# The modulation's sums: one operation of 1024 columns each, and 26 instead of 16 of them in the first feed-forward

## The chip, the cores and the metric

One core of one Trainium2 chip. The metric is the device time of one execution in microseconds, the median of several runs.

## What is computed

Two blocks of a model run one after the other on 256 tokens of width 1024, all in float32. The first block has two layers (pooling and attention, then a gated recurrence), each followed by a feed-forward with a short convolution. The second block has four mixers side by side and a feed-forward, and its two normalised inputs and its two outputs are scaled and shifted by six vectors of width 1024, the modulation, which depend on one row `c` alone:

```python
c_act = jax.nn.silu(c.astype(jnp.float32))
...
mod = (c_act @ ada_w[l] + ada_b[l])[:, None, :]
sh1, sc1, gt1, sh2, sc2, gt2 = jnp.split(mod, 6, axis=-1)
h = rms_norm_2(x, norm_mix_g[l]) * (1.0 + sc1) + sh1
...
x = x + gt1 * (merged @ w_o[l])
h = rms_norm_2(x, norm_ffn_g[l]) * (1.0 + sc2) + sh2
x = x + gt2 * (jnp.square(jax.nn.relu(h @ ffn_w1[l])) @ ffn_w2[l])
```

The product `c_act @ ada_w` has 6144 results of 1024 terms each. It is not made on TensorE: with 128 results on the partitions, 48 columns of sums are made on VectorE (DVE), each the sum of a weight row times `c_act`.

## The kernel before

**Weights.** All weights of the matrix products come in one stream of chunks of 16 tiles of 128 x 128 (1 MB each), loaded by SyncE's queue (`w_dma`, L212) into three buffers. Every product is made in three matmuls of halves of the precision (`mm3`, L276 to L282): high weight by high input, high by low, low by high. The halves of the weights are made on the way (`w_split`, L226): for each 8 tiles ScalarE (ACT) copies the raw weights rounded into `hi` (L246) and DVE subtracts that from the raw ones into `lo` (L247, by the helper L322). There are five pairs of `hi` and `lo` buffers, and the splits run four packages of 8 tiles ahead of their use, `W` (L257) asking for them.

**Order.** The program is one list of work; each engine runs its own part in order. The order among DVE's operations is partly pinned (`behind`, L289): what `step` and `ada_step` issue stays behind what DVE was given before. The stages are mixer 0 (to about 100 us), the first feed-forward (about 100 to 300 us), mixer 1, the second feed-forward (about 390 to 580 us), the four mixers, the last feed-forward. `ffn` (L871) makes 22 groups of 16 tiles; after each, `evac` (L876) applies the convolution, the gelu and the split on ACT and DVE. From the eighth group on, 8 tiles of the output product follow each group, for the group seven before.

**The sums.** `ada_load` (L443) loads 1 MB of modulation weights, two columns of sums, into one of three large buffers, on SyncE's queue, pinned behind what stands there. `ada_step` (L453) makes one column: two scalar_tensor_tensor operations of 512 columns, each with its sum into `macc` (L461). After every second step the next load is issued, but not after steps 28, 30, 32 and 40. `W` calls a step once for every 16 tiles while fewer than `ada_to` steps are done: from the fifth group of the first feed-forward to 16 steps (`ADA_B`, L904), from the fifth group of the second to 32, in the mixers to 38 and 40, in the last feed-forward to 48. `ada_finish` (L468) adds the two halves and the bias for what is used next.

**The set-up of the S5 mixer** (`s5_setup`, L1085) runs in small parts, one for each group of the second feed-forward, called by `step`: small operations on DVE, a Sin on ACT (L1121), six operations of 256 columns on DVE (L1148 to L1150), and once 32 steps of the sums are done, the tables of cosines and sines on GpSimd (POOL, L1170 to L1184), with eight doublings of their length, from 8 to 1024 columns an operation. The tables lie in the three large buffers of the sums' weights. They are read much later, in the mixers.

**Arena.** `al` and `fr` (L162, L179) hand out 46 slots of 512 columns in turn. `start_small` (L512) puts the row `c_act` (doubled) into two of them, which it keeps until the last feed-forward.

Of the kernel before, what the change touches and what calls it, by code (L numbers as in the profile page):

```python
# [12 lines left out]
OP = mybir.AluOpType  # L13
# [11 lines left out]
N_TILES = (128 + 4 + 64 + 2 * (352 + 176) + 160 + 80 + 408 + 3 * 16 + 32 + 64 + 256 + 256)  # L25
TPC = 16
N_CHUNK = -(-N_TILES // TPC)
N_SLOT = 46
MAGIC = 12582912.0
SUM_AT, SPREAD_AT = 6, 2  # L30
SB = 3
# [1 line left out]
STEPS0 = (3, 7)  # L33
ADA_P = 4
SIDE = 4
ADA_B = 16
ADA_M = 38
AHEAD = ((4, 1), (8, 8), (4, 1), (4, 1), (4, 1), (4, 1))
S5_C = 2
# [97 lines left out]
class Prog:  # L137
    def __init__(self, ctx, tc, args):
# [14 lines left out]
        self.uid = self.nsp = 0  # L153
        self.slots = deque(range(N_SLOT))
        self.held = {}
# [120 lines left out]
    def mm3(self, out, key, x, start, stop):  # L276

        wh, wl = self.W(key)
        mm = self.nc.tensor.matmul
        mm(out, wh, x[0], start=start, stop=False, skip_group_check=True)  # L280
        mm(out, wh, x[1], start=False, stop=False, skip_group_check=True)  # L281
        mm(out, wl, x[0], start=False, stop=stop, skip_group_check=True)  # L282

    def mm(self, out, l, r, start=True, stop=True):
        self.nc.tensor.matmul(out, l, r, start=start, stop=stop, skip_group_check=True)  # L285
# [167 lines left out]
    def ada_step(self):  # L453

        i = self.ada_done
        self.ada_done += 1
        raw = self.ada_raw[i // 2]
        with self.behind(*PINNED):
            for h in range(2):
                x = raw[:, (i % 2) * 1024 + h * 512:(i % 2) * 1024 + h * 512 + 512]  # L460
                self.nc.vector.scalar_tensor_tensor(x, x, 0.5, self.cs[h], op0=OP.mult, op1=OP.mult,  # L461
                                                    accum_out=self.macc[:, h, i:i + 1])
        if i % 2 == 1:
            del self.ada_raw[i // 2]
            if self.ada_done not in (28, 30, 32, 40):
                self.ada_load()

    def ada_finish(self, e):  # L468

        while self.ada_done < e:  # L470
            self.ada_step()
        b = self.ada_end
        self.ada_end = e
        c = self.mod[:, b:e]
        self.tt(c, self.macc[:, 0, b:e], self.macc[:, 1, b:e], OP.add)
        self.tt(c, c, self.pvs("adab")[:, b:e], OP.add)


    def start(self):
        nc, a = self.nc, self.a  # L480
        eps, one = self.cst([128, 1], "eps"), self.cst([128, 1], "one")
        nc.vector.memset(eps, EPS)
        nc.scalar.activation(one, eps, AF.Tanh)
        self.eps = eps
        warm = self.al()
        nc.vector.memset(warm[:, :T], 0.0)
        wb = self.bk()
        for _ in range(NWARM):
            self.mm(wb[:, :T], warm[:, :128], warm[:, :T])
        self.bf(wb)  # L490
        self.fr(warm)
        self.pvt = self.cst([128, NPV - PV0], "pvt")
        self.xp = self.cst([128, PV0 + KD * T], "xp")
        self.X = self.xp[:, PV0:].rearrange("p (k t) -> p k t", k=KD)
        p = 0
        for e in (1, 2, 4, 6, 8):
            q = PV0 + e * T
            nc.scalar.dma_start(out=self.xp[:, p:q], in_=a["xt"][:, p:q])
            p = q
        for c in range(self.NRAW):  # L500
            self.w_dma(c)
        cb = self.cst([128, 512], "cb")
        nc.sync.dma_start(out=cb, in_=a["cb"])
        nc.sync.dma_start(out=self.pvt, in_=a["pv"])
        self.ident, self.ones = cb[:, 0:128], cb[:, 128:256]
        self.bd, self.bdm = cb[:, 256:384], cb[:, 384:512]
        self.eps64 = self.cst([128, 1], "eps64")
        nc.vector.memset(self.eps64, 64e-5)
        self.xgh = self.cst([128, KD, T + 4], "xgh", F32R)
        self.macc, self.mod = self.cst([128, 2, 48], "macc"), self.cst([128, 48], "mod")  # L510

    def start_small(self):  # L512

        self.cs = []
        th = self.al()
        for h in range(2):
            c = self.al()
            self.nc.sync.dma_start(out=c, in_=self.a["crow"][:, h * 512:h * 512 + 512].to_broadcast([128, 512]))
            self.nc.scalar.activation(th, c, AF.Tanh, scale=0.5)
            self.stt(c, th, 1.0, c, OP.add, OP.mult)  # L520
            self.cs.append(c)
        self.fr(th)


# [346 lines left out]
    def ffn(self, l):  # L871
# [29 lines left out]
        for p, b in self.in_gen(specs, hs):  # L901
            evac(p, b)
            if p == ADA_P:
                self.ada_to = (ADA_B, 32)[l]  # L904
            if p == SIDE:
# [872 lines left out]
    def ffn2(self):  # L1778
        nc = self.nc
        hs = []  # L1780
        b3 = (128, 2, T)
        ys = {}
        specs = [[("ffn1", 2 * q), ("ffn1", 2 * q + 1)] for q in range(16)]

        def evac(q, b):
            r = self.al()
            nc.scalar.activation(r, b, AF.Relu)
            self.rel(b)
            h, l = self.al(F32R), self.al(F32R)
            nc.scalar.activation(h, r, AF.Square)  # L1790
            self.tt(r, r, r, OP.mult)
            self.tt(l, r, h.bitcast(F32), OP.subtract)
            self.fr(r)
            ys[q] = (h, l)

        def xk(q, i):
            return tuple(t[:, i * T:i * T + T] for t in ys[q])
        gate = lambda m: self.mod[:, 40 + m:41 + m]

        def out(q):  # L1800
            if q == 0:
                self.acc_begin()
            for i in range(2):
                self.out_k("ffn2", 2 * q + i, xk(q, i), q == 0 and i == 0)
            self.fr(*ys.pop(q))
        for q, b in self.in_gen(specs, hs):
            evac(q, b)
            if q == 4:
                self.ada_load(3)
                self.ada_to = 48  # L1810
            if LAG2 <= q and q - LAG2 < 16 - LAST2:
                out(q - LAG2)
        self.fr(*hs)
        for q in range(16 - LAG2, 16 - LAST2):
            out(q)
        self.ada_finish(48)
        self.fr(*self.cs)

        self.tb = [[self.bk() for _ in range(2)] for _ in range(2)]

        def turn(m):
            x = self.al()
            nc.scalar.activation(x[:, :T], self.X[:, m, :], AF.Copy, scale=self.pv("gfin", m))
            for h in range(2):
                nc.tensor.transpose(self.tb[h][m // 4][:, (m % 4) * 128:(m % 4) * 128 + 128],  # L1825
                                    x[:, h * 128:h * 128 + 128], self.ident)
            self.fr(x)
        with self.behind(ENG.Activation):
            self.nc.scalar.activation(self.cst([128, 1], "sqrt"), self.eps, AF.Sqrt)
        last = range(16 - LAST2, 16)  # L1830
        self.out_last("ffn2", range(32 - 2 * LAST2, 32), [xk(q, i) for q in last for i in range(2)], gate=gate,
                      after=turn)
        for q in last:
            self.fr(*ys.pop(q))
# [149 lines left out]
```

## Time and profile before

| | us |
|---|---|
| median of three runs | 1043.2 |
| lowest and highest | 1041.69 and 1044.56 |
| the profiled execution | 1046.05 |
| its span, first to last instruction | 1044.3 |
| TensorE (PE) busy | 1015.2 |
| DVE busy | 865.7 |
| ACT busy | 605.3 |
| POOL busy | 96.8 |

The granted clock of TensorE is 0.995 of full speed over the span, the 2.4 GHz level. A busy time counts an engine's instructions from start to end; consecutive ones can overlap a little. A wait in the profile is idle time of an engine just before an instruction, put down to what released it. Lines such as L322 and L331 are helpers that many places call, so tiles tell more: `lo<-raw,hi` is a split, `ada<-ada,s` a sum, `tab` a table, `s` an arena slot, `b` a PSUM bank.

### The profile page before, as it was taken

What the parts mean: (1) busy time and instruction counts of PE and PEld (TensorE: products, weight loads), DVE (VectorE), ACT (ScalarE), POOL (GpSimd) and SP (SyncE); (2) the same over time, 40 slices, a digit from 0 to 9 for tenths busy, and PEclk for the clock granted to TensorE, in tenths of its full rate; (3) what the DMA queues carried; (4) which work ended last, traced back from release to release, by engine and by line L of the source; (5) the groups of instructions that cost most, each with busy time, mean ns of one, the idle gap of its engine ahead of it and who ended that gap; (6) DMA issues with size and microseconds to landing.
All of it is one profiled execution on the core that took longest, in us unless ns stands there. A gap on an engine that the chain in (4) does not pass through costs nothing. (4 is left out here: it accounts for less than half of the span.)

```text
span 1044.3 us, 21508 instructions
## 1 busy us (share of the span) xinstructions
PE 1015.2 (97%) x8834; PEld 980.9 (94%) x8834; DVE 865.7 (83%) x1662; ACT 605.3 (58%) x953; POOL 96.8 (9%) x86
## 2 busy tenths in 40 slices
PE   9999999999999999999999999889999999999996
PEld 8879999999999999999999998778999999999996
DVE  6887999997799998999999978997667979775554
ACT  6566665565669975665654687233345457444444
POOL 0000000000000000000295000334200200000000
PEclk9999999999999999999999999999999999999999
DMA  8953367886682263777654644234454464955531
GB/s 310 353 186 119 125 207 272 305 314 223 211 281 95 71 235 120 241 255 269 225 202 153 241 149 149 72 116 146 145 198 162 154 206 142 386 172 192 191 133 41
DMA packets 32499, 202.75 MB, mean 194 GB/s; under 512 B 3601, under 2 KB 5137, under 8 KB 9233
## 3 DMA queue, kind: packets, MB, share of 16 engines
q1 hardware_dynamic: 31392, 199.80, 54.2%
q10 hardware_dynamic: 1008, 1.58, 0.4%
q8 instruction: 69, 1.13, 0.4%
q14 instruction: 30, 0.24, 0.1%
HBM read 200.32 MB, written 1.05 MB: 193 GB/s over the span
## 5 line engine op out<-in xcount | busy, mean ns | idle before, releaser
L281 PE MATMUL b<-s,hi 128*128 128x256 f32 x2192 | 616.9, 282 | 1.8 <-DVE s L331 0.9
L280 PE MATMUL b<-s,hi 128*128 128x256 f32 x2128 | 600.6, 283 | 4.8 <-ACT s L342 3.0
L282 PE MATMUL b<-s,lo 128*128 128x256 f32 x2128 | 598.2, 282 | 4.1 <-DVE lo L322 4.0
L322 DVE TENSOR_TENSOR lo<-raw,hi 128x1024 fp32r<-128x1024 f32 (+1 forms) x309 | 389.8, 1266 | 112.1 <-ACT hi L246 111.2
L246 ACT CAST hi<-raw 128x1024 fp32r<-128x1024 f32 (+1 forms) x309 | 319.8, 1041 | 261.4 <-PE b L281 185.4
L281 PEld LDWEIGHTS b<-s,hi 128*128 128x128 f32 x2192 | 413.4, 189 | 6.0 <-issue 3.0
L280 PEld LDWEIGHTS b<-s,hi 128*128 128x128 f32 x2128 | 400.6, 189 | 12.2 <-issue 4.0
L282 PEld LDWEIGHTS b<-s,lo 128*128 128x128 f32 x2128 | 400.9, 189 | 6.8 <-DVE lo L322 5.8
L322 DVE TENSOR_TENSOR s<-s,s 128x256 f32<-128x256 f32 (+3 forms) x173 | 89.2, 524 | 8.0 <-ACT s L373 3.7
L331 DVE SCALAR_TENSOR_TENSOR s<-b,pvt,s 128x255 f32<-128x255 f32 (+1 forms) x153 | 72.6, 478 | 3.8 <-ACT s L880 2.8
L461 DVE SCALAR_TENSOR_TENSOR ada<-ada,s 128x512 f32<-128x512 f32 x96 | 63.9, 685 | 3.6 <-DMA ada<-in_ada_dram 3.6
L285 PE MATMUL b<-xgh,hi 128*128 128x256 f32 (+1 forms) x212 | 60.5, 285 | 0.0
L285 PE MATMUL b<-s,hi 128*128 128x256 f32 x212 | 59.6, 281 | 0.0
L285 PE MATMUL b<-xgh,lo 128*128 128x256 f32 (+1 forms) x212 | 59.6, 281 | 0.0
L342 ACT CAST s<-s 128x256 fp32r<-128x256 f32 (+1 forms) x77 | 33.0, 440 | 37.0 <-DVE s L322 26.6
L880 ACT ACTIVATE s<-b,pvt 128x256 f32<-128x256 f32 x76 | 42.0, 556 | 8.5 <-PE b L282 8.2
L285 PE MATMUL b<-s,s 128*128 128x256 f32 (+5 forms) x212 | 39.2, 380 | 7.9 <-DVE s L322 7.4
L1174 POOL MEMSET tab<- 128x8 f32 x1 | 0.1, 113 | 494.2 <-DVE ada L461 494.2
L285 PEld LDWEIGHTS b<-s,hi 128*128 128x128 f32 x212 | 40.1, 189 | 0.0
L285 PEld LDWEIGHTS b<-xgh,lo 128*128 128x128 f32 x212 | 40.0, 189 | 0.0
L285 PEld LDWEIGHTS b<-xgh,hi 128*128 128x128 f32 x212 | 39.9, 188 | 0.0
L322 DVE TENSOR_TENSOR s<-s 128x256 f32<-128x256 f32 (+3 forms) x70 | 35.4, 508 | 4.7 <-ACT s L1790 4.3
(367 smaller groups left out, 1042.3 us busy)
## 6 DMA issues: line engine op xcount, KB each, us to landing
raw<-in_wst_dram SPq DMA_DIRECT2D x157, 1024.0 KB, 5.0
ada<-in_ada_dram SPq DMA_DIRECT2D x24, 1024.0 KB, 7.4
raw<-in_wst_dram SPq DMA_DIRECT2D x4, 512.0 KB, 6.4
s<-in_catt_dram SPq DMA_DIRECT2D x8, 192.0 KB, 7.2
s<-in_rgw_dram SPq DMA_DIRECT2D x5, 256.0 KB, 3.7
raw<-in_wst_dram SPq DMA_DIRECT2D x4, 256.0 KB, 5.5
xp<-in_xt_dram ACTq DMA_DIRECT2D x3, 256.0 KB, 6.1
s<-in_cinv_dram SPq DMA_DIRECT2D x2, 256.0 KB, 5.5
```

Source lines behind the costliest of these rows:

```text
L246: self.nc.scalar.copy(h, s)
L280: mm(out, wh, x[0], start=start, stop=False, skip_group_check=True)
L281: mm(out, wh, x[1], start=False, stop=False, skip_group_check=True)
L282: mm(out, wl, x[0], start=False, stop=stop, skip_group_check=True)
L285: self.nc.tensor.matmul(out, l, r, start=start, stop=stop, skip_group_check=True)
L322: self.nc.vector.tensor_tensor(out, a, b, op=op)
L331: self.nc.vector.scalar_tensor_tensor(out, a, s, b, op0=op0, op1=op1)
L342: nc.scalar.copy(hi, src)
L461: self.nc.vector.scalar_tensor_tensor(x, x, 0.5, self.cs[h], op0=OP.mult, op1=OP.mult, accum_out=self.macc[:, h, i:i + 1])
L880: nc.scalar.activation(c[:, i, :], z, AF.Identity, scale=self.pv(f"fcw{l}2", m), bias=self.pv(f"fcb{l}", m))
L1174: g.memset(S[:, :, 0:1], 0.0)
```

## The change

Each step makes one operation of 1024 columns with one sum, instead of two of 512; `macc` has one column a step, and the addition of the halves goes. The row `c_act` lies in one buffer of 1024 columns outside the arena, which has 44 slots instead of 46. `ADA_B` is 26: the first feed-forward makes steps 0 to 25, and the second 26 to 31. All sixteen loads that were issued up to step 26 are so issued in the first feed-forward, and the second issues none.

```diff
-N_SLOT = 46
+N_SLOT = 44
...
-ADA_B = 16
+ADA_B = 26
...
         with self.behind(*PINNED):
-            for h in range(2):
-                x = raw[:, (i % 2) * 1024 + h * 512:(i % 2) * 1024 + h * 512 + 512]
-                self.nc.vector.scalar_tensor_tensor(x, x, 0.5, self.cs[h], op0=OP.mult, op1=OP.mult,
-                                                    accum_out=self.macc[:, h, i:i + 1])
+            x = raw[:, (i % 2) * 1024:(i % 2) * 1024 + 1024]
+            self.nc.vector.scalar_tensor_tensor(x, x, 0.5, self.cs, op0=OP.mult, op1=OP.mult,
+                                                accum_out=self.macc[:, i:i + 1])
...
-        self.tt(c, self.macc[:, 0, b:e], self.macc[:, 1, b:e], OP.add)
-        self.tt(c, c, self.pvs("adab")[:, b:e], OP.add)
+        self.tt(c, self.macc[:, b:e], self.pvs("adab")[:, b:e], OP.add)
...
-        self.macc, self.mod = self.cst([128, 2, 48], "macc"), self.cst([128, 48], "mod")
+        self.macc, self.mod = self.cst([128, 48], "macc"), self.cst([128, 48], "mod")
...
-        self.cs = []
+        self.cs = self.cst([128, 1024], "cs")
         th = self.al()
         for h in range(2):
-            c = self.al()
+            c = self.cs[:, h * 512:h * 512 + 512]
...
-            self.cs.append(c)
...
-        self.fr(*self.cs)
```

## Rows read from the trace of the kernel before

**Rows 1.** busy time of the engines over the whole span

```profile
PE 1015.2 (97%) x8834; PEld 980.9 (94%) x8834; DVE 865.7 (83%) x1662; ACT 605.3 (58%) x953; POOL 96.8 (9%) x86
```

**Rows 2.** by stretch, us: busy PE, PEld, DVE, ACT, POOL; clock, DMA share

```profile
160.00:226.00 66.00, 66.00 (x559) 66.00 (x560) 65.16 (x142) 37.86 (x57) 0.00 (x0) 1.00 0.83 294
...
226.00:280.00 54.00, 54.00 (x459) 54.00 (x459) 41.56 (x62) 31.34 (x46) 0.00 (x0) 1.00 0.68 234
...
458.00:494.00 36.00, 34.71 (x290) 34.10 (x289) 33.90 (x87) 22.50 (x33) 0.00 (x0) 1.00 0.79 274
...
537.00:565.00 28.00, 28.00 (x239) 28.00 (x239) 27.58 (x22) 12.03 (x17) 26.47 (x14) 1.00 0.45 155
```

**Rows 3.** what PE waited for, 120 to 300 us (total, times, longest)

```profile
PE b L282 <- DVE lo L322: 1.3, 1, 1.3
```

**Rows 4.** the same view, 400 to 580 us

```profile
PE b L282 <- DVE lo L322: 1.7, 3, 0.9
...
PE b L280 <- ACT s L342: 1.0, 1, 1.0
...
PE b L281 <- DVE s L322: 0.7, 1, 0.7
```

**Rows 5.** timeline of DVE, second feed-forward: start us, us, engine, line

```profile
461.84 1.22 DVE L322 TENSOR_TENSOR lo<-raw,hi 128x1024 fp32r<-128x1024 f32 x1
462.97 0.48 DVE L331 SCALAR_TENSOR_TENSOR s<-b,pvt,s 128x254 f32<-128x254 f32 x1
463.36 0.68 DVE L461 SCALAR_TENSOR_TENSOR ada<-ada,s 128x512 f32<-128x512 f32 x1
...
463.97 0.69 DVE L461 SCALAR_TENSOR_TENSOR ada<-ada,s 128x512 f32<-128x512 f32 x1
...
464.58 1.22 DVE L322 TENSOR_TENSOR lo<-raw,hi 128x1024 fp32r<-128x1024 f32 x1
```

**Rows 6.** timeline: two splits on DVE and the matmul that first uses each

```profile
459.07 1.22 DVE L322 TENSOR_TENSOR lo<-raw,hi 128x1024 fp32r<-128x1024 f32 x1
...
460.83 0.28 PE L282 MATMUL b<-s,lo 128*128 128x256 f32 x1
...
491.36 1.22 DVE L322 TENSOR_TENSOR lo<-raw,hi 128x1024 fp32r<-128x1024 f32 x1
...
494.49 0.28 PE L282 MATMUL b<-s,lo 128*128 128x256 f32 x1
```

**Rows 7.** timeline: last sum of the sixth step; the Sin that the tables read

```profile
458.18 0.69 DVE L461 SCALAR_TENSOR_TENSOR ada<-ada,s 128x512 f32<-128x512 f32 x1
...
462.75 0.33 ACT L1121 ACTIVATE s5sa<-s5sa 128x144 f32<-128x144 f32 x1
```

**Rows 8.** timeline of POOL: memset of the cosines, a middle and the last table operation

```profile
514.88 0.11 POOL L1173 MEMSET tab<- 128x8 f32 x1 [9.77 <-DVE ada L461]
...
545.95 2.88 POOL L1179 TENSOR_TENSOR tab<-tab,s5sa 128x1024 f32<-128x1024 f32 x1
...
561.41 2.45 POOL L1184 TENSOR_TENSOR tab<-tab,tab 128x1024 f32<-128x1024 f32 x1
```

**Rows 9.** timeline of DVE and PE beside the tables

```profile
540.83 1.82 DVE L322 TENSOR_TENSOR lo<-raw,hi 128x1024 fp32r<-128x1024 f32 x1
...
551.24 0.28 PE L282 MATMUL b<-s,lo 128*128 128x256 f32 x1
...
543.59 1.49 DVE L322 TENSOR_TENSOR s<-s 128x256 f32<-128x256 f32 x1
...
561.53 3.41 DVE L322 TENSOR_TENSOR lo<-raw,hi 128x1024 fp32r<-128x1024 f32 x1
...
565.44 0.28 PE L282 MATMUL b<-s,lo 128*128 128x256 f32 x1
```

**Rows 10.** timeline of DVE: first and last of six operations of the set-up

```profile
484.73 0.42 DVE L322 TENSOR_TENSOR s<-s,s5qr 128x256 f32<-128x256 f32 x1
...
487.88 0.42 DVE L322 TENSOR_TENSOR s<-s,s 128x256 f32<-128x256 f32 x1
```

## The prediction

> **What bounds the kernel now.** I read the busy line first. TensorE is busy for 1015.2 of the 1044.3 us of the profiled span [rows 1], so the whole stock of idle PE time is some 29 us, and an edit on another engine can only move what PE waits for. The waits of PE come next, in the two stretches where the sums of the modulation lie: 1.3 us in the first feed-forward [rows 3], and 1.7, 1.0 and 0.7 us around the second [rows 4]. Then the busy time by stretch: beside the sums DVE is busy for 65.16 of 66 us and PE still runs without a gap; after them, 226 to 280 us, DVE is busy for 41.56 of 54 [rows 2]. The last thing I read is how early DVE delivers. DVE makes the low half ("lo") of eight weight tiles at a time; PE uses such a package in 24 matmuls. 459 matmuls in 54 us are 118 ns each [rows 2], so a package lasts 2.83 us and a step of the sums (every 16 tiles) comes every 5.65 us. The **lead** is the time from the end of a lo to the first matmul that loads it; I found that matmul by counting every eighth lo matmul back or on from one that waited for its lo. When the lead is used up, PE stops, one for one.
>
> **The operation itself.** Two halves of 512 columns start 0.61 us apart, and 0.61 us after the second the next work starts [rows 5]: 1.22 us a step, the reading of the accumulator included. The nearest row to one operation of 1024 columns with two SBUF operands is the lo itself: 1.13 us from its start to that of the next [rows 5]. I add 0.01 for the accumulator and take 1.14, with 1.13 and 1.22 as ends. That saves 0.08 us in each of 48 steps, 3.8 us of DVE time, at most a few tenths on the path: PE waits for DVE near few of these steps. The Trainium skill speaks against this form: "Vector Engine (DVE) Microarchitecture Reference", section "Points that are easy to get wrong", says that a scalar_tensor_tensor with two SBUF sources that are not bf16 runs at half throughput. The trace disagrees: a half of 512 columns takes 0.61 us where 1024 columns of the lo take 1.13, the same rate. By the rule a step would be 2.3 us and ten more would overfill the first feed-forward; I give it 1 in 100.
>
> **First feed-forward.** It gets ten more steps, 10 x 1.14 = 11.4 us of DVE work over 56.5 us, in the stretch where DVE idled for 12.4 of 54 us [rows 2]. It becomes as full as 160 to 226 us was, where PE lost nothing [rows 2]. So I cost it at nothing; the cover is the 12.4 us of idle DVE time, and what is left over is 1.0 us. If it is too thin, the nearest price is the 1.3 us that PE lost where the sums met the small set-up of the next mixer [rows 3]. The steps bring five loads of 1 MB with them, which move here from the second feed-forward. Each waits on SP's queue for the second sum of its pair, with the weight loads queued behind it. That is the pattern of 160 to 226 us too, at a DMA share of 0.83 against 0.68 after it [rows 2], without a wait of PE: nothing. The 1.3 us in this part I leave standing.
>
> **Second feed-forward.** It keeps six steps of sixteen. Ten steps of 1.22 us leave DVE. What PE lost there falls into two parts: 0.9 us at 484 and 0.4 at 488 us, where the sums met the set-up of the S5 tables on DVE (two of the three waits that make the 1.7), and 1.0 + 0.7 us at its end, where DVE came late out of the building of the tables [rows 4]. The third, the other 0.4, lies before the first step and stays. So 3.0 us can be won.
>
> But the sums also hold back **POOL**. The sine and cosine tables are written into the very buffers that the sums read, and POOL's memset of the cosines, behind which all but three tiny table operations stand, waited for the last sum of the sixteenth step, until 514.88 us [rows 8]. With six steps that sum ends near 458.9 us, and the tables then wait only for the Sin that they read, which ends at 463.08 us [rows 7]. So the tables start some 51.8 us earlier, and run through 463 to 512 us where they ran from 515 to 564. That matters, because beside POOL's operations the operations of DVE that read two SBUF operands stretch: a lo took 1.82 and 3.41 us instead of 1.22, and one of 256 columns 1.49 instead of 0.42 [rows 9, 10]. The Trainium skill has this rule: "SBUF — State Buffer", section "Who interferes with whom", says that a DVE instruction with two SBUF inputs and a GpSimd instruction that reads SBUF contend, and that the second to issue blocks until the first ends. The trace agrees: a lo of 1.22 us took 3.41 while POOL's operations of 2.45 and more ran.
>
> The lead, step by step. (1) The lo that ends at 460.29 us is used at 460.83: 0.54 us. The lo that ends at 492.58 is used at 494.49: 1.91 us [rows 6]. Between them PE waited 1.3 us [rows 4], so DVE just kept pace (1.91 - 0.54 - 1.3 = 0.07) while it did five steps of 1.22 us, the sums of 463.4 to 489 us. Without these 6.1 us the lead at the same place is 0.54 + 0.07 + 6.1 = 6.7 us, had POOL been quiet. (2) POOL's operations of 256 and 512 columns now fall there (they ran in the 15 us up to 545.95). Ordinary DVE work paid some five times 0.6 us for them (the lo of 540.83 [rows 9]): 3.0. The set-up's six operations of 256 columns, at 484.7 to 488.3 us [rows 10], now stand beside them too. No row shows these two together; the ends are nothing (they slip ahead of the larger operations) and 6 x 1.07 = 6.4 us (each paying as the one at 543.59 [rows 9]). Three of the six lie, shifted, among the 512-column operations; at 0.6 to 1.07 us each I take 2.6. Lead before the largest operations: 6.7 - 3.0 - 2.6 = 1.1 us, with 3.7 and below zero as ends. (3) The operations of 1024 columns: before, the lo that ended at 542.65 was used at 551.24, a lead of 8.6; the one that ended at 564.94 was used at 565.44, a lead of 0.5 [rows 9]. They cost 8.1 us, and a full lead just carried it. With 1.1 us of lead, PE waits 7.0 us, some time in 495 to 520 us; the ends are 8.1 - 3.7 = 4.4 and 8.1 + 6.4 - 3.7 = 10.8.
>
> After that DVE has neither sums nor POOL beside it, catches up in the rest of this part, and the last 1.7 us of waiting go. What is late next is nothing new: the end of the second feed-forward runs as that of the first did, with no wait of PE [rows 3].
>
> **The rest.** The row of conditioning values moves from two arena slots to a buffer of its own while the arena loses two: 44 slots are free either way from there on. One addition of at most 32 columns goes from each of four finishes. In the mixer and the second half of the model the steps stay where they were, 0.08 us shorter. All nothing, with 0.3 us either way.
>
> **Sum.** Waits lost 3.0, waits gained 7.0: +4.0 us. The profiled execution took 1046.05 us, its span 1044.3; by its own time the changed kernel would take 1050.1. It lies 2.85 us above the median of the three timed runs, 1043.2, so on that scale I forecast **1047.2 us**, with 1044.6 to 1051.0 from the ends. A measurement of this kernel can tell about 0.3%, 3.1 us, from no change: the bounds are 1040.1 and 1046.3.
>
> **Rivals.** (a) *The lead is full before the tables get heavy.* If the relieved DVE climbs to some 8 us of lead by 494 us, as it had in 537 us, it pays the 8.1 us from that and PE waits for almost nothing: 1043.2 - 3.0 = 1040.2, and some tenths less with the shorter operations. For it: DVE loses 6.1 us of work there. Against it: six set-up operations and the smaller POOL operations eat 3 to 6 of that. It decides at a lead of 8 us. (b) *Half of it.* The set-up slips ahead of the larger operations and PE waits 3 to 4.4 us: 1043.2 to 1044.6. (c) *The tables don't start earlier*, because POOL waits for something that the sums hid. Then only the 1.3 us at 484 and 488 us go and the end stays as it is: 1041.9. The trace shows nothing for such a wait, nor can it. (d) *The first feed-forward overflows*: the leftover of 1.0 us of idle DVE time is too little, weights come late, and PE pays 1.3 us or more there, on top of the forecast: 1048.5.
>
> **How the numbers follow.** Forecast 0.48 (a quarter of it under 1046.3), (a) 0.14, (b) 0.17, (c) 0.11, (d) 0.09, the half-rate operation 0.01. Slower by over 0.3%: three quarters of 0.48, and (d) and the half rate, 0.46, and a little for what no row shows: 0.49. Faster by over 0.3%: most of (a), 0.10. Within: 0.41. The range leaves out the ends of (a) and of the forecast: 1040.6 to 1050.0.
>
> **What would show it.** Right: the table operations on POOL from about 463 us; lo operations of 2 to 3.4 us in 494 to 512; a wait of PE for lo of some 7 us in 485 to 520; none at 565 to 570; PE without a gap in 226 to 280 with DVE busy for about 53 of 54 us; one sum of about 1.2 us by its duration, 48 of them. Wrong: POOL starting after 500 us, or the large table operations met by a lead of 8 us, or a new wait of PE at the end of the first feed-forward.

## The result, and the profile after

The changed kernel takes 1050.81 us (median of 13 runs, 1047.39 to 1056.07); the kernel before, run beside it on the same chip, 1044.56 us (13 runs, 1041.58 to 1048.48). The ratio is 1.0063, with 1.0049 to 1.0077 as its 95% interval: slower by some 6.6 us. The forecast was slower by 4.0 us, 1047.2; the time lies above the upper end of the range, 1050.0. (By the ratio alone it would be 1043.2 x 1.0063 = 1049.8 on the scale of the forecast, at the very end of the range.) The profiled execution of the changed kernel took 1051.49 us, its span 1049.7, 5.4 more than before.

The first lines of the page, and its group of the sums:

```profile
span 1049.7 us, 21408 instructions
...
PE 1018.3 (97%) x8834; PEld 985.2 (94%) x8834; DVE 862.9 (82%) x1563; ACT 605.3 (58%) x953; POOL 93.2 (9%) x86
...
L460 DVE SCALAR_TENSOR_TENSOR ada<-ada,cs 128x1024 f32<-128x1024 f32 x48 | 58.4, 1216 | 3.8 <-DMA ada<-in_ada_dram 3.8
```

DVE has 99 instructions and 2.8 us less than in [rows 1], and there are 48 sums of 1.22 us, as the change says. PE has the same 8834 matmuls and is busy 3.1 us *longer*. That is the first sign of something that the waits of PE will not show. The waits of PE, in 120 to 300, 300 to 400 and 400 to 600 us (total, times, longest), answer [rows 3, 4]:

```profile
PE b L280 <- DVE xp L322: 1.0, 1, 1.0
...
PE b L285 <- DVE s L322: 0.7, 1, 0.7
...
PE b L282 <- DVE lo L322: 4.1, 3, 2.7
PE b L280 <- ACT hi L246: 1.0, 1, 1.0
```

The wait of 1.3 us at 158 us is gone; two new ones of 1.0 and 0.7 stand at 290 and 301 us, where the first feed-forward ends and mixer 1 begins. In the second feed-forward PE waits 5.1 us, where it waited 3.4 [rows 4]. The busy time by stretch, with the columns of [rows 2]:

```profile
160.00:226.00 66.00, 66.00 (x561) 66.00 (x560) 64.89 (x118) 38.19 (x57) 0.00 (x0) 1.00 0.84 303
226.00:280.00 54.00, 54.00 (x459) 54.00 (x458) 47.92 (x77) 29.13 (x44) 0.00 (x0) 1.00 0.84 301
280.00:302.00 22.00, 20.28 (x171) 19.89 (x169) 20.51 (x38) 18.45 (x35) 0.00 (x0) 1.00 0.77 281
460.00:496.00 36.00, 36.00 (x308) 36.00 (x307) 36.00 (x65) 20.27 (x30) 31.63 (x43) 1.00 0.60 209
494.00:503.00 9.00, 6.31 (x53) 6.10 (x53) 9.00 (x10) 2.70 (x5) 8.92 (x5) 1.00 0.21 77
503.00:506.42 3.42, 3.42 (x18) 3.42 (x17) 3.42 (x3) 0.00 (x0) 3.34 (x2) 0.50 0.83 287
506.42:513.25 6.83, 4.37 (x33) 3.75 (x32) 6.12 (x7) 2.75 (x4) 3.54 (x2) 1.00 0.02 10
513.25:516.66 3.41, 3.41 (x18) 3.41 (x18) 3.30 (x7) 2.06 (x4) 0.00 (x0) 0.50 0.81 257
516.66:530.00 13.34, 13.34 (x114) 13.34 (x114) 13.13 (x21) 10.25 (x16) 0.00 (x0) 1.00 0.74 252
```

Read the column of the clock, last but two: right behind each stretch in which PE stood still (6.31 of 9 us, then 4.37 of 6.83) the granted clock is 0.50, the 1.2 GHz level, for 3.41 us. PE counts as busy for all of it. The timeline of PE, two matmuls inside the first fall and two behind it, gives the price:

```profile
504.09 0.41 PE L281 MATMUL b<-s,hi 128*128 128x256 f32 x1
504.30 0.41 PE L282 MATMUL b<-s,lo 128*128 128x256 f32 x1
...
506.55 0.28 PE L281 MATMUL b<-s,hi 128*128 128x256 f32 x1
506.67 0.28 PE L282 MATMUL b<-s,lo 128*128 128x256 f32 x1
```

Inside the fall a matmul starts every 0.213 us, outside every 0.118 us. Sixteen start in a fall (the 18 of the view count those that reach in from its ends), so each fall costs some 1.5 us, and the two 3.0 us. The kernel before has no such fall between 120 and 600 us.

POOL, from its memset of the cosines on, answers [rows 8] (timeline: start us, us, engine, line):

```profile
459.73 0.11 POOL L1170 MEMSET tab<- 128x8 f32 x1 [23.29 <-DVE ada L460]
463.36 0.21 POOL L1176 TENSOR_TENSOR tab<-tab,s5sa 128x8 f32<-128x8 f32 x1 [3.52 <-DMA raw<-in_wst_dram]
...
499.35 2.08 POOL L1179 TENSOR_TENSOR tab<-tab,s5sa 128x1024 f32<-128x1024 f32 x1
501.38 3.35 POOL L1178 TENSOR_TENSOR tab<-tab,tab 128x1024 f32<-128x1024 f32 x1
504.81 1.90 POOL L1180 TENSOR_TENSOR tab<-tab,s5sa 128x1024 f32<-128x1024 f32 x1
506.79 3.25 POOL L1181 TENSOR_TENSOR tab<-tab,tab 128x1024 f32<-128x1024 f32 x1
```

and DVE beside it, which answers [rows 9, 10]:

```profile
483.19 2.02 DVE L322 TENSOR_TENSOR s<-s,s 128x256 fp32r<-128x256 f32 x2
...
491.17 0.89 DVE L322 TENSOR_TENSOR mod<-macc,pvt 128x32 f32<-128x32 f32 x1
...
499.59 2.91 DVE L322 TENSOR_TENSOR lo<-raw,hi 128x1024 fp32r<-128x1024 f32 x1
502.43 0.47 DVE L331 SCALAR_TENSOR_TENSOR s<-b,pvt,s 128x255 f32<-128x255 f32 x1
502.82 1.94 DVE L358 CAST xgh<-mod 128x8 fp32r<-128x8 f32 x1
504.67 0.47 DVE L331 SCALAR_TENSOR_TENSOR s<-b,pvt,s 128x254 f32<-128x254 f32 x1
505.07 2.72 DVE L322 TENSOR_TENSOR lo<-raw,hi 128x1024 fp32r<-128x1024 f32 x1
507.71 2.61 DVE L322 TENSOR_TENSOR s<-s 128x256 f32<-128x256 f32 x1
```

Lay the two over each other. The lo of 499.59 ends at 502.50, 1.07 us after the POOL operation that was running when it came (499.35 + 2.08 = 501.43). The lo of 505.07 ends at 507.79, 1.08 us after its POOL operation (506.71). The CAST of eight columns a partition ends at 504.76, 0.03 us after its own (504.73), and the operation of 507.71 ends 0.28 us after 510.04. So each of them waits for the whole rest of the POOL operation in front of it and then takes its ordinary time. In the operations of 254 and 255 columns, which read one operand from PSUM, nothing stretches: 0.47 us.

By matching the same matmul in both traces, the 5.4 us of span arise so. At the start of the second feed-forward the changed kernel is 1.84 us behind; at its end (613.85 us before, 620.59 after) 6.74; the rest gives 1.3 back. The second feed-forward thus costs 4.9: waits 5.1 instead of 3.4, so 1.7; two falls of the clock, 3.0; 0.2 that I can't assign. The 1.84 ahead of it are 1.0 + 0.7 of new waits, less the 1.3 at 158 us, and 1.5 of a fall of the clock at 62.7 us (together 1.9). That fall is not the change's: nothing is changed there, and it comes and goes among the traces of this study (7 of 13 have it, one of them of a kernel that runs as the kernel before up to 493 us).

### The profile page after: what moved, and what is told of

It reads as the page before. It is cut to its first block, busy times and chain, and to the rows that moved or that the text cites. A ratio compares the mean times of both kernels' runs of the same rounds, so it can differ in the third digit from the quotient of the medians.

```text
span 1049.7 us, 21408 instructions
## 1 busy us (share of the span) xinstructions
PE 1018.3 (97%) x8834; PEld 985.2 (94%) x8834; DVE 862.9 (82%) x1563; ACT 605.3 (58%) x953; POOL 93.2 (9%) x86
## 3 DMA queue, kind: packets, MB, share of 16 engines
q8 instruction: 69, 1.13, 0.4%
## 5 line engine op out<-in xcount | busy, mean ns | idle before, releaser
L322 DVE TENSOR_TENSOR s<-s,s 128x256 fp32r<-128x256 f32 (+3 forms) x173 | 87.6, 514 | 6.3 <-ACT s L373 3.7
L460 DVE SCALAR_TENSOR_TENSOR ada<-ada,cs 128x1024 f32<-128x1024 f32 x48 | 58.4, 1216 | 3.8 <-DMA ada<-in_ada_dram 3.8
L322 DVE TENSOR_TENSOR s<-s 128x256 f32<-128x256 f32 (+3 forms) x70 | 37.7, 541 | 4.5 <-ACT s L1787 4.2
```

The lines of the kernel that those rows point to most:

```text
L322: self.nc.vector.tensor_tensor(out, a, b, op=op)
L460: self.nc.vector.scalar_tensor_tensor(x, x, 0.5, self.cs, op0=OP.mult, op1=OP.mult, accum_out=self.macc[:, i:i + 1])
```

## The experiments

My theory: the relieved sums let POOL build the tables inside the busiest part of the second feed-forward, DVE is held up by each large POOL operation, and PE stops. Against it stood that the added steps in the first feed-forward, or the operation of 1024 columns, cost the time. Waits are those of PE in the profiled execution, us; falls those of the granted clock between 490 and 530 us.

| | us | ratio to before | 120–300 | 300–400 | 400–600 | falls |
|---|---|---|---|---|---|---|
| before | 1043.7 to 1044.6 | 1 | 1.3 | 0 | 3.4 | 0 |
| changed | 1050.81 | 1.0063 (1.0049–1.0077) | 1.0 | 0.7 | 5.1 | 2 |
| e1 one operation, 16 steps | 1042.95 | 0.9988 (0.9975–1.0000) | 0 | 0 | 1.4 | 0 |
| e2 two halves, 26 steps | 1052.04 | 1.0080 (1.0060–1.0101) | 2.3 | 0.7 | 6.0 | 2 |
| e4 no tables | 1042.69 | 0.9986 (0.9975–0.9997) | 1.2 | 0.7 | 0 | 0 |
| e3 tables late, failed | 1048.34 | 1.0046 (1.0029–1.0062) | 0.8 | 0.7 | 5.6 | 2 |
| e7 tables late | 1042.42 | 0.9986 (0.9977–0.9996) | 0.3 | 0.7 | 0 | 0 |
| e5 tables in pieces | 1042.46 | 0.9983 (0.9971–0.9994) | 0.3 | 0.7 | 0 | 0 |
| e8 pieces, 16 steps | 1040.64 | 0.9974 (0.9964–0.9985) | 0 | 0 | 0 | 0 |
| e6 before, with pieces | 1041.82 | 0.9979 (0.9968–0.9990) | 0 | 0 | 0.4 | 0 |
| e10 pieces, 22 steps | 1041.68 | 0.9980 (0.9970–0.9991) | 0 | 0 | 0 | 0 |
| e9 finish kept in place | 1049.35 | 1.0055 (1.0035–1.0075) | 0.3 | 0.7 | 3.5 | one, 6.8 us |
| e11 no set-up operations | 1044.96 | 1.0011 (1.0001–1.0022) | 0 | 1.1 | 2.4 | 0 |

The runs of e1 to e5 and e7 to e9 had a kernel before of 1043.7 us beside them, those of e6, e10 and e11 one of 1044.11; compare by the ratio.

**Which part of the change (e1, e2).** e1 is the changed kernel with 16 steps:

```diff
-ADA_B = 26
+ADA_B = 16
```

> The changed kernel with 16 steps in the first feed-forward again: the one operation of 1024 columns, the row outside the arena and 44 slots stay. Theory T (the loss comes from the S5 tables on POOL, which start 50 us earlier when only six steps are left in the second feed-forward): ratio to before 0.998 to 1.001, the tables start at about 515 us, PE waits near 484 and near 568 us as before. Rival R1 (the longer operation or the moved row delays DVE): ratio 1.004 to 1.008.

e2 is the kernel before with 26:

```diff
-ADA_B = 16
+ADA_B = 26
```

> The kernel before with 26 steps in the first feed-forward and the two halves kept. Theory T: ratio 1.004 to 1.008, the tables start near 463 us and PE waits 4 to 7 us between 490 and 515. Rival R1: ratio 0.998 to 1.002.

e1 takes 0.9988 of before, e2 1.0080. The whole loss is in the move of the ten steps; the operation of 1024 columns is at most a small gain, for its interval reaches 1.0000. e1's waits did not stay where I expected them: the 1.4 us lie at 450, 456 and 567 us, and none near 484.

**Are the tables the cost (e4)?** The changed kernel fills both tables with constants and leaves the doublings on POOL out (its scan is not the model's):

```diff
-        g.memset(C[:, :, 0:1], 1.0)
-        g.memset(S[:, :, 0:1], 0.0)
-        for n in range(8):
+        g.memset(C[:, :, :], 1.0)
+        g.memset(S[:, :, :], 0.0)
+        for n in range(0):
```

> The changed kernel with the tables set by two memsets of their whole length; the doublings on POOL are left out. Theory T: no wait of PE from 430 to 600 us, ratio 0.995 to 0.999, and no fall of the granted clock near 500 us. Rival R2: ratio 1.003 to 1.007.

0.9986, no wait of PE in the second feed-forward and no fall of the clock there. So the tables in their new place cost 1.0063 - 0.9986 = 0.0077, 8.0 us (give or take 1.9, by the two intervals), and all the rest of the change is worth 1.5 us.

**Is it where they run (e3, e7)?** e3 wanted to hold the tables back with a small POOL operation that reads a late result of the feed-forward:

```diff
+            self.last_x = x[:, 0, :8].bitcast(F32)
...
+        late = self.cst([128, 8], "late")
+        g.tensor_tensor(late, self.last_x, self.last_x, op=OP.mult)
...
         g.memset(C[:, :, 0:1], 1.0)
```

> The changed kernel, but POOL must read an input of the output product of the group just evacuated before it builds the tables, so that they start near 510 us again; the 26 steps stay in the first feed-forward. Theory T: the waits of PE at 495 to 515 us go, none or less than 2 us at the end of the second feed-forward, ratio 0.996 to 1.001. Rival R2 (the fuller first feed-forward, or the order of DVE's work, costs the time): ratio stays at 1.004 to 1.007.

It failed as an experiment: nothing tied the tables to that operation, the memsets and the doublings went ahead of it, and the tables started at 462.46 us, the operation only at 516.00. What it gives is the changed kernel a second time, 1.0046. e7 keeps the order on POOL:

```diff
+            self.last_x = x[:, 0, :8].bitcast(F32)
...
-        g.memset(C[:, :, 0:1], 1.0)
-        g.memset(S[:, :, 0:1], 0.0)
+        late = self.cst([128, 8], "late")
+        g.tensor_tensor(late, self.last_x, self.last_x, op=OP.mult)
+        with self.behind(ENG.Pool):
+            g.memset(C[:, :, 0:1], 1.0)
+            g.memset(S[:, :, 0:1], 0.0)
```

> The changed kernel, with a small POOL operation that reads the input of the output product of the group last evacuated, and both memsets of the tables pinned behind it, so that the tables start near 510 us as before the change. Theory T (the early tables cost the time): the lead is full when they start, PE waits at most 1.5 us between 400 and 600 us, the clock stays at its upper level there, ratio to before 0.999 to 1.002 (the waits of some 1.7 us about 290 to 310 us stay). Rival R2 (26 steps in the first feed-forward cost it): ratio 1.004 to 1.007.

POOL in e7:

```profile
502.18 0.11 POOL L1174 MEMSET tab<- 128x8 f32 x1
...
528.36 2.87 POOL L1180 TENSOR_TENSOR tab<-tab,s5sa 128x1024 f32<-128x1024 f32 x1
...
543.81 2.46 POOL L1185 TENSOR_TENSOR tab<-tab,tab 128x1024 f32<-128x1024 f32 x1
```

The same table work, 39 us later: 0.9986, no wait of PE in 400 to 600 us, no fall of the clock. The start lay some 8 us earlier than I had expected, and the ratio a little lower. With the 26 steps in place, the whole loss hangs on when the tables run.

**Is it their length (e5)?** The same multiplications from the same start, but no POOL operation above 256 columns:

```diff
-            ecn = ec[:, n * 8:n * 8 + 8].unsqueeze(2).to_broadcast([128, 8, w])
...
-            g.tensor_tensor(C[:, :, w:2 * w], C[:, :, :w], ecn, op=OP.mult)
...
+            q = max(1, w * 8 // 256)
+            for i in range(q):
+                r = slice(i * 8 // q, (i + 1) * 8 // q)
+                ecn = ec[:, n * 8:n * 8 + 8][:, r].unsqueeze(2).to_broadcast([128, 8 // q, w])
...
+                g.tensor_tensor(C[:, r, w:2 * w], C[:, r, :w], ecn, op=OP.mult)
...
```

> The changed kernel with every table operation of 512 and 1024 columns cut into pieces of 256; the tables start early as in the changed kernel. If an operation of DVE waits for the POOL operation that runs and not for the tables as a whole, no lo beside them takes over 2 us, PE waits less than 2 us between 400 and 600 us, ratio 0.999 to 1.002. If the work of POOL slows DVE in proportion, nothing changes: lo of 3 us, ratio 1.004 to 1.008.

The splits on DVE in 494 to 508 us, and the stretch 494 to 512 us by engine:

```profile
495.54 1.30 DVE L322 TENSOR_TENSOR lo<-raw,hi 128x1024 fp32r<-128x1024 f32 x1
...
499.09 1.63 DVE L322 TENSOR_TENSOR lo<-raw,hi 128x1024 fp32r<-128x1024 f32 x1
...
501.55 1.43 DVE L322 TENSOR_TENSOR lo<-raw,hi 128x1024 fp32r<-128x1024 f32 x1
...
504.27 1.75 DVE L322 TENSOR_TENSOR lo<-raw,hi 128x1024 fp32r<-128x1024 f32 x1
```

```profile
494.00:512.00 18.00, 18.00 (x155) 18.00 (x154) 17.79 (x26) 10.05 (x16) 18.00 (x18) 1.00 0.60 197
```

POOL is busy for all of the 18 us, and PE runs without a gap at the full clock. A lo takes at most 1.75 us where it took 2.9. The tables end at 522.6 us instead of 510.0, which nobody waits for. DVE still pays for POOL's work, but in small pieces: its lead over PE stays above 3.6 us from 490 us to the end of the tables. Ratio 0.9983, a little below what I expected: the loss is the length of the single POOL operation, not the amount of POOL's work.

**The set-up's share (e11).** The ledger of the prediction charged 2.6 us to six operations of 256 columns that now stand beside the tables. The changed kernel without them (so that, again, its scan is not the model's):

```diff
-        bb, tm = self.al(shape=(128, 2, 8, 32)), self.al(shape=(128, 2, 8, 32))
...
-            self.tt(bb[:, i], bb[:, i], tm[:, i], OP.subtract if i == 0 else OP.add)
-        self.fr(tm, bl)
+        bb = bl
```

> The changed kernel without the six set-up operations of 256 columns at the head of the second feed-forward (the kernel leaves out what they compute, so its scan is not the model's). The ledger charged them against TensorE's lead with 2.6 us. If that term is right, the waits for lo in 400 to 600 us shrink from 5.1 us to about 2.5, and the ratio from 1.006 to about 1.002 to 1.004, one fall of the clock fewer among them. If the lead was spent by the large table operations alone, the waits stay near 5 us and only VectorE's 2 us of work go: ratio 1.005 to 1.006.

```profile
PE b L282 <- DVE lo L322: 2.4, 2, 2.2
```

That is all of PE's waits in 400 to 600 us: 2.7 less than in the changed kernel. The ratio falls by 0.0052, 5.4 us, to 1.0011, below the expected 1.002 to 1.004 and by twice as much as the waits: both falls of the clock went with them (3.0). Waits and falls, 5.7 us, make up the time within the intervals. The experiment takes away the operations' own time on DVE as well as what they paid beside POOL, so it does not measure the ledger's 2.6 alone.

**The end of the feed-forward (e9).** The last sum's finish moved forward on DVE to where POOL was heavy (the addition of 491.17, the CAST of 502.82). e9 keeps three of its operations at their place in the order:

```diff
-            self.ada_finish(32)
...
+            with self.behind(*PINNED):
+                self.ada_finish(32)
...
```

> The changed kernel with the finish of the modulation's first 32 columns and the two small operations on it pinned at their place in the list, behind the evacuation of the last group; in the changed kernel they ran beside the largest table operations and took 0.9 to 1.9 us each. Theory T2 (these operations, which the forecast did not count, are about 3 us of the wait): PE waits 2 to 3.5 us instead of 5.1 between 400 and 600 us, ratio 1.002 to 1.005. If they don't matter: 1.005 to 1.008.

PE waits 3.5 us in one piece (505.7 to 509.2) instead of 5.1, but the clock falls within that wait, at 507.7, and stays at its lower level for 6.8 us, and the ratio, 1.0055, can't be told from the changed kernel's. Inconclusive for the time.

**The first feed-forward (e10), and the best of both (e8, e6).** e10 is e5 with 22 steps first:

```diff
-ADA_B = 26
+ADA_B = 22
```

> The changed kernel with the tables in pieces of 256 columns and 22 instead of 26 steps in the first feed-forward. If the waits at the end of the first feed-forward (0.3 to 1.0 us at 290 and 0.7 at 301) come from the ten added steps, they vanish with four of them gone, the second feed-forward still shows none, and the ratio is 0.996 to 0.9975. If they come from elsewhere they stay, and the ratio is that of the pieces with 26 steps, 0.998 to 0.999.

The two waits at 290 and 301 us vanish with the four steps, as they are absent in every kernel with 16 and present, the one or the other, in every kernel with 26. The time does not tell: 0.9980 against 0.9983, and it missed what I expected. e8 is e5 with 16 steps, e6 the kernel before with the pieces of e5:

> One operation of 1024 columns, 16 steps in the first feed-forward, and the table operations in pieces of 256 columns. Theory T: the 0.4 us at the end of the second feed-forward goes too, the waits near 484 us stay; ratio 0.996 to 0.999. If the pieces do nothing, 0.998 to 1.000.

> The kernel before (two operations of 512 columns, 16 steps first) with the tables' operations in pieces of 256 columns. If the 1.7 us of waits at the end of its second feed-forward come from the length of the table operations beside lo, they go, and the 1.3 us at 158 and those near 484 and 488 stay: ratio 0.998 to 0.999. If they come from VectorE's sums alone, they stay: 0.9995 to 1.001.

e8 has the lowest time of the study, 1040.64 us, and PE waits for nothing between 120 and 600 us, though I expected the waits near 484 us to stay. Its interval overlaps those of e5, e6 and e10, so that it is the best of them is not shown. e6 takes 0.9979; the 1.7 us of waits at its end are gone, and what is left, 0.4 us, lies at 418 us, before the first step. But its waits at 158 and near 484 us are gone too, against my expectation: up to 493 us e6 gives its engines the same instructions in the same order as the kernel before, and PE waited 1.3 + 1.3 us there in the one profiled execution and not at all in the other. That the move to one operation adds anything to e6 is not shown (0.9974 against 0.9979).

## Why the prediction was right and wrong, step by step

**The operation of 1024 columns: right.** The next operation starts 1.14 us after the sum of 458.44 us, the reading of the accumulator included; 1.14 was taken:

```profile
458.44 1.22 DVE L460 SCALAR_TENSOR_TENSOR ada<-ada,cs 128x1024 f32<-128x1024 f32 x1
459.58 0.09 DVE L460 DVE_READ_ACCUMULATOR ada<-ada,cs 128x1 f32 x1
459.58 0.42 DVE L322 TENSOR_TENSOR s<-s 128x256 f32<-128x256 f32 x1
```

The half rate that the Trainium skill states ("Vector Engine (DVE) Microarchitecture Reference", "Points that are easy to get wrong") would by estimate, twice the 1.13 us of a lo, have made it 2.3 us; the 48 sums took 1216 ns each on the mean, and the trace stands against the page for this operand pair.

**First feed-forward at nothing: wrong in small.** PE lost 1.0 + 0.7 us at its end, which the prediction had named as a sign of being wrong. DVE was not too full: it was busy for 47.92 of the 54 us from 226 to 280, not the 53 that I had forecast, and between 226 and 290 us it waited 5.7 us for hi. What failed is the sentence on the loads, "the pattern of 160 to 226 us too [...]: nothing". The pattern fits inside the stretch, but not at its end, where the first weights of mixer 1 queue behind the added loads. ACT, in the changed kernel:

```profile
279.94 1.14 ACT L246 CAST s<-raw 128x512 fp32r<-128x512 f32 x2 [2.98 <-DMA raw<-in_wst_dram]
```

Before, it waited at most 0.7 us for a load between 226 and 295 us. In all eight kernels with 26 steps the longest such wait was 1.6 to 3.3 us; in all five with 16 or 22, at most 0.7. e10 shows that four of the steps make the two waits of PE; that it is their loads rather than their sums is the reading of this row and was not tried alone. The place was that of rival (d), and so was the late weight, but not its reason, a DVE without idle time; its price was 1.3, and 1.7 was measured in the trace.

**The waits that I left standing or counted as won: a size taken from one execution.** I won 3.0 us in the second feed-forward and kept 1.3 at 158 us. By e4 and e7 the change without its tables is worth 1.5 us. The new waits at the end of the first feed-forward (1.2 us in the trace of e4, 0.9 in that of e7) could explain most of the difference; but e6 shows that 1.3 of the 3.0, and the 1.3 at 158, are not there in another execution of the same instructions. The times don't tell the two apart. A wait of a microsecond in a single profile is no stock to be won.

**The tables' start: right.** 463 us was forecast, 463.36 measured; their last operation ends at 510.0, forecast 512. Rival (c) fell with it. e7 builds late tables as in (c), and the time agrees: 1041.9 forecast, 0.9986 x 1043.2 = 1041.7 measured. That is luck in part, for (c) kept the 1.7 us of waits at the end, which e7 does not have, and had none at the end of the first feed-forward, where e7 waits 0.9 us.

**The ledger of the lead: right in kind, too large by 1.9 us.** PE's waits were 5.1 us, forecast 7.0 (ends 4.4 to 10.8). The term that was mis-sized is the lead before the largest operations. It can be read at the package of weights of [rows 6] (the lo of 491.36 there), first without the tables, in e4, then in the changed kernel:

```profile
483.97 1.22 DVE L322 TENSOR_TENSOR lo<-raw,hi 128x1024 fp32r<-128x1024 f32 x1
...
493.49 0.28 PE L282 MATMUL b<-s,lo 128*128 128x256 f32 x1
```

```profile
489.18 1.67 DVE L322 TENSOR_TENSOR lo<-raw,hi 128x1024 fp32r<-128x1024 f32 x1
...
494.06 0.28 PE L282 MATMUL b<-s,lo 128*128 128x256 f32 x1
```

Without the tables the lead is 8.3 us (493.49 less 485.19), where I had 6.7 for a quiet POOL. With the tables it is 3.2, where I had 1.1. So the relief of DVE was 1.6 larger than I took it, and the smaller table operations and the set-up beside them cost 5.1 instead of 5.6. The six set-up operations took 4.5 us in all instead of 2.5, so 2.0 more, forecast 2.6. From a lead of 3.2 the ledger's 8.1 for the largest operations leaves a wait of 4.9. In e7, where the largest operations meet a lead of 9.0 us, they do take 8.1 of it:

```profile
523.63 1.43 DVE L322 TENSOR_TENSOR lo<-raw,hi 128x1024 fp32r<-128x1024 f32 x1 [0.47 <-ACT hi L246]
...
534.07 0.28 PE L282 MATMUL b<-s,lo 128*128 128x256 f32 x1
...
543.94 3.42 DVE L322 TENSOR_TENSOR lo<-raw,hi 128x1024 fp32r<-128x1024 f32 x1
...
548.26 0.29 PE L282 MATMUL b<-s,lo 128*128 128x256 f32 x1
```

That 4.9 comes so near to 5.1 is luck in part: the finish of the sums (0.89 and 1.94 us among its operations) was not counted, and the first fall of the clock, in which PE used weights more slowly, gave DVE some 1.5 us. Rival (a), a lead of 8 us, was not reached, and (b), waits of 3 to 4.4, was nearer to the waits than the forecast was, yet it would have given a time well below the measured one. That contradiction leads to the step that was missing.

**The missing step: what a stall of PE costs behind it.** I priced a stall at its own length, "PE stops, one for one". Four stalls of 0.7 to 2.7 us cost the 5.1 us that PE stood, and behind them came twice 3.41 us at half the clock. The two falls are 3.0 us, more than half as much again as the waits, and no view of waits shows them, since PE counts as busy. e11 (5.4 us gained from 2.7 of waits) bears it out. The early tables cost 5.1 + 3.0 = 8.1 us by the trace and 8.0 by the ratios.

So the sum as measured is -1.5 + 8.0 = +6.5, where mine was -3.0 + 7.0 = +4.0. Of the 2.5 us between them, 1.5 are a gain that was not there and 1.0 the price of the tables, in which a wait that was too large by 1.9 hid most of a clock of 3.0 that was left out. The upper end of the range was too low: the working had 1051.0 as the end from the bounds of the unknown costs and left its last microsecond out, and the clock stood in none of its cases. Another 1.4 us of the distance from 1047.2 to 1050.8 are not the change's: the forecast starts from a kernel before of 1043.2, a median of three, and beside the changed kernel it took 1044.56.

## What to carry to other kernels

Before work is taken off an engine, look at which other engine was held back by it through shared buffers: moving the sums moved POOL's tables by 52 us into the busiest stretch. Where two engines contend by whole operations, cut the operations of the one that has time (256 instead of 1024 columns took all the waits of the second feed-forward away; POOL's tables ended 12.6 us later, and no time was lost by it), and do so before moving anything. Price a stall of PE with a case in which the clock falls behind it, and don't count a wait of 1 us from one profile as won until another execution shows it too.

## What the runs showed of the hardware that I had not expected

- DVE and POOL took turns by whole operations: a DVE operation beside POOL waited for the rest of the running POOL operation and then took its ordinary time (ends 1.07, 1.08, 0.28 and 0.03 us behind POOL's). What DVE pays is set by the length of POOL's operation, not by its own: eight columns waited as long as 1024. The Trainium skill ("SBUF — State Buffer", "Who interferes with whom") says of DVE operations in a two-port mode that whoever issues first gets the pair of ports shared with GpSimd for the whole instruction and blocks the other. The trace agrees, and shows the same for the splits, which read two inputs (1.07 and 1.08 us behind POOL's end).
- Operations of DVE with one SBUF operand were held as well: the CAST of 128x8 took 1.94 us, and in e11 a TENSOR_SCALAR of 128x256, 0.28 us otherwise, took this:

```profile
502.82 1.98 DVE L326 TENSOR_SCALAR s<-s 128x256 f32<-128x256 f32 x1
```

  The same section of the Trainium skill names cast and tensor_scalar among the operations that can take both ports. The forecast had counted only operations with two operands.
- Behind PE's wait of 2.7 us, and again behind waits of 0.7, 1.0 and 0.8 us in 507 to 513, the granted clock fell to 0.50 for 3.41 us each. The waits of 1.0 and 0.7 at 290 and 301 us left it at 1.00, and so did one of 2.2 us in e11; one of 1.8 us at 161 to 163 us in e2 was followed by 3.41 us at 0.50, and within one of 3.5 us in e9 it fell for 6.8 us. What decides it is left open; the size of a single wait does not.
